# Decoder trunk on one core: gates and mixer up-projections with tokens on the output partitions, and raw buffers of their own for chunks loaded out of turn

## The chip, the cores and the metric

The kernel runs on one core of a Trainium2 chip. The metric is the device time of one execution in microseconds, as the median of several runs. The engines are named as in the profile: PE (matrix multiply; PEld is its weight load), DVE (vector), ACT (scalar), POOL, and SP, whose queue starts most transfers.

## What is computed

Two layers of a decoder trunk over 256 tokens, `D_MODEL` 2048, all in float32. The reference, cut to the part around the change:

```python
def hybrid_mixer(x, ...):
    q, k, v, u = ...                                # x @ w_in, 1024 columns each
    gate_a = jax.nn.sigmoid(x @ w_in[:, OFF_GA:OFF_GS])   # 2048 columns
    gate_s = jax.nn.sigmoid(x @ w_in[:, OFF_GS:])         # 2048 columns
    attn = diff_attention(rope(q), rope(k), v, ...)       # (256, 1024)
    ssm = s5_ssm(u, ..., w_glu)                           # (256, 1024)
    merged = gate_a * (attn @ w_attn_up) + gate_s * (ssm @ w_ssm_up)
    return merged @ w_out

for l in range(2):
    x = layer_norm(ALPHA * x + hybrid_mixer(x, ...), ...)
    h = square(relu(x @ w_mlp_up[l])) @ w_mlp_down[l]
    x = layer_norm(ALPHA * x + h, ...)
```

## The kernel before

Every weight matrix is streamed once from device memory in chunks of 256 input rows by 512 columns (512 KB), laid out as [128, 2, 512]: two k-tiles of 128 rows. A list `plan` holds all chunks in the order of use. `load` takes a raw buffer (tag `w`, 4 buffers), starts the transfer on SP's queue (L344), and has the chunk split into a high and a low part in float32r: ACT writes `hi` (L142), DVE the remainder `lo` (L144). `hi` and `lo` have 3 buffers each. Activations are kept split in the same way, so that one float32 product is three float32r products: high by high, high by low, low by high.

There are two forms of a product with 512 output columns. Both do the same multiplications on a chunk and the same number of PE columns, 6144:

- `gemm_feat` puts features on the output partitions. The weights are the stationary operand, the 256 tokens move: 24 matmuls of 256 columns on a chunk (L532 to L534). The result is [128 features, 256 tokens], in the layout in which the next product takes its activations.
- `gemm_tok` puts tokens on the output partitions (`tok_mul`, L457, L458, L461). The activations are stationary, 128 tokens at a time, and the 512 weight columns move: 12 matmuls of 512 columns on a chunk. The result is [128 tokens, 512 features], once for each half `tt` of the tokens.

A layer runs: `u`, `q`, `k` (feat), `v` (tok), eight gate products (feat, 8 chunks each), four of `w_attn_up` (feat, 4 chunks each), two of `w_glu` (feat), four of `w_ssm_up` (feat, 4 chunks each), `w_out` (tok), a first MLP product (`w_mlp_head`, tok), `w_mlp_up` (`gemm_up`, a third form, L555) and `w_mlp_down` (tok). The gates' evacuation is a tanh on ACT (L968). That of `w_attn_up` (`gate_attn`, L975) multiplies on DVE; that of `w_ssm_up` (`merge`, L1007, L1008, then the split at L142 and L146) makes `merged`, the activations of `w_out`, straight in the layout that `w_out` takes.

Attention and the state-space scan run as background generators on DVE, ACT and a little PE, beside these products: after each chunk, `bg.pump(rate[0])` hands out so many microseconds of background work by the program's own estimate, and `AW` is the share that attention gets against the scan. Whatever attention has left when the gates' products are issued is issued then (`bg.finish(agen)`). A scheduler then places the instructions on each engine.

At the end of `w_out` and of the last `w_mlp_down` of a layer the order of chunks is changed: the last 5 (at the very end 8) chunks of the last product and 2 chunks of the next matrix are taken out of `plan` by `reserve` and loaded ahead, during the two products before (n = 1 and 2, 16 chunks of their own). After each chunk `stash_next` calls `load(own=True)`: the same four raw buffers, but a `whl` slot of its own for `hi` and `lo` (tag `slot`, 17 buffers of 8 KB for each partition, shared with most long-lived tiles). `boundary` and `gemm_tail` use them later. `hold` makes an instruction wait until the last matmul of the most recent chunk is done, and `drip_next` starts a queued POOL transfer (L447) at such a point.

The parts that the change touches:

Of the kernel before, what the change touches and what calls it, by code (L numbers as in the profile page):

```python
# [12 lines left out]
F32R = mybir.dt.float32r  # L13
# [3 lines left out]
ALU = mybir.AluOpType  # L17
# [21 lines left out]
HL_BUFS = 3  # L39
AHEAD = 1  # L40
RATE = (2.0, 1.8)
AW = 1.5
TAIL = 5
LAST = 8
LEAD = 3
# [59 lines left out]
def trunk(ctx: ExitStack, tc: tile.TileContext, A, out):  # L105
# [230 lines left out]
    plan = []  # L336
    ready = []

    def load(w, c, own=False, halves=False):
        kn, wn = w.shape[-2:]  # L340
        raw = wpool.tile([P, kn, wn], F32, tag="w", name=nm("w"), bufs=RAW_BUFS)
        parts = [slice(0, 1), slice(1, 2)] if halves else [slice(0, kn)]
        for k in parts:
            nc.sync.dma_start(raw[:, k], w[c][:, k])  # L344
        if own:
            hl = slot([P, 2, 2, W], F32R, "whl")
            hi, lo = hl[:, 0], hl[:, 1]
        else:
            hi = wpool.tile([P, kn, wn], F32R, tag="whi", name=nm("whi"), bufs=HL_BUFS)
            lo = wpool.tile([P, kn, wn], F32R, tag="wlo", name=nm("wlo"), bufs=HL_BUFS)  # L350
        for k in parts:
            split(hi[:, k], lo[:, k], raw[:, k])
        return hi, lo
# [13 lines left out]

    stash = []
    stashed = {}

    def reserve(w, chunks):
        for c in chunks:
            i = next(i for i, (w_, c_) in enumerate(plan) if w_ is w and c_ == c)
            stash.append(plan.pop(i))

    def stash_next():
        if stash:
            w, c = stash.pop(0)
            stashed[id(w), c] = load(w, c, own=True)

    def take(w, c):
        while any(w_ is w and c_ == c for w_, c_ in stash):
# [80 lines left out]
    def gemm_tok(w, act, nkt, evac, tail=0):  # L463
        ps = banks([P, W])
        nch = nkt // 2
        for c in range(nch - tail):
            hl = take(w, c)
            mm = Chain()
            for tt in range(2):
                tok_mul(mm, ps, act, nkt, hl, c, tt)  # L470
            drip_next(mm.last)
            stash_next()
            bg.pump(rate[0])
        if not tail:
            for tt in range(2):
                evac(tt, ps[tt])
        return ps
# [433 lines left out]
    for l in range(DEPTH):  # L911
# [50 lines left out]
        for base in (G_GS, G_GA):  # L962
            for n in range(4):
                if n % 2 == 0:
                    gt = slot([P, 2, 4, 256], name="gate")
                g = gates[base, n] = gt[:, n % 2]
                gemm_feat(weights("w_in", l, base + n), act, NKT,
                          lambda b, ps: SC.activation(g[:, 2 * b:2 * b + 2, :], ps, AF.Tanh, scale=0.5))  # L968
        bg.finish(agen)
        aact = from_tiles(st["attn"])  # L970
        for n in range(4):
            def gate_attn(b, ps):
                g = gates[G_GA, n][:, 2 * b:2 * b + 2, :]
                with tc.high_priority():
                    V.scalar_tensor_tensor(g, g, 1.0, ps, op0=ALU.add, op1=ALU.mult)  # L975

            gemm_feat(weights("w_attn_up", l, n), aact, 8, gate_attn)
        bg.finish(sgen)
        ghl = []
        for i in range(2):  # L980
# [20 lines left out]
        for n in range(4):  # L1001
            merged.append(slot([P, 4, 2, 256], F32R, "merged"))

            def merge(b, ps):
                bs = slice(2 * b, 2 * b + 2)
                mt = t_fg([P, 2, 256])
                V.scalar_tensor_tensor(mt, gates[G_GS, n][:, bs, :], 1.0, ps, op0=ALU.add, op1=ALU.mult)  # L1007
                V.tensor_tensor(mt, mt, gates[G_GA, n][:, bs, :], op=ALU.add)  # L1008
                split(merged[n][:, bs, 0, :], merged[n][:, bs, 1, :], mt, scale=0.5)

            gemm_feat(weights("w_ssm_up", l, n), sact, 8, merge)
        mact = from_tiles(merged)
        assert not drip
        xgen = None
# [160 lines left out]
```

## Time and profile before

| | before |
|---|---|
| median of 3 runs | 2741.55 us (2741.41 to 2743.21) |
| the profiled execution | 2731.09 us |
| its span, first to last instruction | 2729.3 us |
| PE busy / weight loads busy | 98% / 87% of the span |
| DVE / ACT / POOL busy | 70% / 48% / 5% |
| read from device memory | 513.32 MB |
| mean moved, read and written | 195 GB/s |
| mean granted TensorE clock | 0.994 |

Spans and rows come from the one profiled execution, 10.5 us below the median. A busy share is the union of an engine's instructions. A PE matmul's duration contains its way through the array, which overlaps with the next one, so the distance between starts is what a matmul costs when PE is full.

### The profile page before, as it was taken

What the parts mean: (1) busy time and instruction counts of PE and PEld (TensorE: products, weight loads), DVE (VectorE), ACT (ScalarE), POOL (GpSimd) and SP (SyncE); (2) the same over time, 40 slices, a digit from 0 to 9 for tenths busy, and PEclk for the clock granted to TensorE, in tenths of its full rate; (3) what the DMA queues carried; (4) which work ended last, traced back from release to release, by engine and by line L of the source; (5) the groups of instructions that cost most, each with busy time, mean ns of one, the idle gap of its engine ahead of it and who ended that gap; (6) DMA issues with size and microseconds to landing.
All of it is one profiled execution on the core that took longest, in us unless ns stands there. A gap on an engine that the chain in (4) does not pass through costs nothing. (4 is left out here: it accounts for less than half of the span.)

```text
span 2729.3 us, 41597 instructions
## 1 busy us (share of the span) xinstructions
PE 2676.5 (98%) x16384; PEld 2371.8 (87%) x16384; DVE 1908.7 (70%) x2675; ACT 1312.6 (48%) x1755; POOL 147.1 (5%) x274
## 2 busy tenths in 40 slices
PE   7999999999999999999999999999999999999997
PEld 7889999988888888888789899999788888888876
DVE  6899988676765566655657998987776655556555
ACT  4554555454554454443444555544445544435442
POOL 3100000000000010000012000001000000000000
PEclk9999999999999999999999999999999999999999
DMA  8755555663655676655657555557746555555573
GB/s 262 224 187 188 174 173 169 212 234 122 220 190 192 205 237 212 220 198 195 227 167 253 185 179 171 166 179 230 252 135 205 187 194 191 190 195 186 193 234 121
DMA packets 158675, 536.04 MB, mean 196 GB/s; under 512 B 27504, under 2 KB 27536, under 8 KB 158480
## 3 DMA queue, kind: packets, MB, share of 16 engines
q1 hardware_dynamic: 133344, 482.40, 53.2%
q0 software_dynamic: 25136, 50.99, 6.6%
q8 instruction: 128, 2.10, 0.3%
q14 instruction: 67, 0.55, 0.1%
HBM read 513.32 MB, written 19.92 MB: 195 GB/s over the span
## 5 line engine op out<-in xcount | busy, mean ns | idle before, releaser
L144 DVE TENSOR_TENSOR wlo<-w,whi 128x1024 fp32r<-128x1024 f32 (+1 forms) x884 | 1078.3, 1221 | 660.3 <-ACT whi L142 655.3
L142 ACT ACTIVATE whi<-w 128x1024 fp32r<-128x1024 f32 (+1 forms) x884 | 934.3, 1058 | 1085.3 <-PE g L461 425.6
L555 PE MATMUL g<-xT,whi 128*128 128x512 f32 x1920 | 655.7, 395 | 2.3 <-ACT whi L142 2.3
L532 PE MATMUL g<-xT,whi 128*128 128x256 f32 x1792 | 509.3, 287 | 11.8 <-ACT whi L142 11.8
L533 PE MATMUL g<-xT,whi 128*128 128x256 f32 x1792 | 508.5, 286 | 0.0
L534 PE MATMUL g<-xT,wlo 128*128 128x256 f32 x1792 | 500.0, 287 | 7.1 <-DVE wlo L144 7.0
L555 PE MATMUL g<-xT,wlo 128*128 128x256 f32 x1920 | 497.7, 280 | 0.2 <-DVE wlo L144 0.2
L555 PEld LDWEIGHTS g<-xT,whi 128*128 128x128 f32 x1920 | 344.9, 188 | 66.9 <-ACT whi L142 2.6
L458 PE MATMUL g<-wlo,hT 128*128 128x512 f32 x972 | 379.4, 390 | 3.6 <-DVE wlo L144 3.5
L555 PEld LDWEIGHTS g<-xT,wlo 128*128 128x128 f32 x1920 | 362.1, 189 | 21.7 <-DVE wlo L144 1.4
L457 PE MATMUL g<-whi,hT 128*128 128x512 f32 x972 | 379.1, 390 | 0.9 <-ACT whi L142 0.9
L532 PEld LDWEIGHTS g<-xT,whi 128*128 128x128 f32 x1792 | 347.9, 194 | 14.7 <-ACT whi L142 12.9
L534 PEld LDWEIGHTS g<-xT,wlo 128*128 128x128 f32 x1792 | 341.8, 194 | 10.2 <-DVE wlo L144 9.6
L533 PEld LDWEIGHTS g<-xT,whi 128*128 128x128 f32 x1792 | 347.9, 194 | 1.0 <-issue 0.8
L461 PE MATMUL g<-whi,hT 128*128 128x512 f32 x972 | 300.3, 390 | 0.0
L458 PEld LDWEIGHTS g<-wlo,hT 128*128 128x128 f32 x972 | 182.7, 188 | 43.9 <-DVE wlo L144 5.7
L457 PEld LDWEIGHTS g<-whi,hT 128*128 128x128 f32 x972 | 182.9, 188 | 39.6 <-ACT whi L142 2.1
L461 PEld LDWEIGHTS g<-whi,hT 128*128 128x128 f32 x972 | 182.9, 188 | 38.0
L458 PE MATMUL g<-wlo,merged 128*128 128x512 f32 x216 | 85.3, 395 | 3.4 <-DVE wlo L144 3.2
L560 ACT ACTIVATE at<-g 128x256 f32<-128x256 f32 x120 | 43.8, 384 | 87.3 <-PE g L555 87.3
L457 PE MATMUL g<-whi,merged 128*128 128x512 f32 x216 | 84.4, 391 | 0.0
L710 DVE TENSOR_TENSOR_SCAN sw<-ss,sw 128x512 f32<-128x512 f32 x64 | 75.7, 1212 | 0.0
(290 smaller groups left out, 3186.1 us busy)
## 6 DMA issues: line engine op xcount, KB each, us to landing
w<-in_w_mlp_down_dram SPq DMA_DIRECT2D x256, 512.0 KB, 3.3
w<-in_w_in_dram SPq DMA_DIRECT2D x255, 512.0 KB, 3.4
w<-in_w_mlp_up_dram SPq DMA_DIRECT2D x240, 512.0 KB, 3.3
w<-in_w_out_dram SPq DMA_DIRECT2D x64, 512.0 KB, 4.3
w<-in_w_attn_up_dram SPq DMA_DIRECT2D x32, 512.0 KB, 3.3
w<-in_w_ssm_up_dram SPq DMA_DIRECT2D x32, 512.0 KB, 4.3
w<-in_w_glu_dram SPq DMA_DIRECT2D x16, 512.0 KB, 3.2
w<-in_w_mlp_head_dram SPq DMA_DIRECT2D x16, 512.0 KB, 3.5
```

The lines of the kernel that those rows point to most:

```text
L142: SC.activation(hi, src, AF.Copy, scale=scale)
L144: V.tensor_tensor(lo, src, hi.bitcast(F32), op=ALU.subtract)
L457: mm(PE.matmul(ps[tt], act(kt)[:, 0, ts], hi[:, k, :], start=kt == 0, stop=False))
L458: mm(PE.matmul(ps[tt], act(kt)[:, 0, ts], lo[:, k, :], start=False, stop=False))
L461: mm(PE.matmul(ps[tt], act(kt)[:, 1, ts], hi[:, k, :], start=False, stop=kt == nkt - 1))
L532: m(PE.matmul(o, wh, ah, start=first and b % 2 == 0, stop=False))
L533: m(PE.matmul(o, wh, al, start=False, stop=False))
L534: m(PE.matmul(o, wl, ah, start=False, stop=last and b % 2 == 1))
L555: mm[j](PE.matmul(o, wt, mv, start=kt == 0 and i == 0, stop=last and i == 1))
L560: SC.activation(r[:, j], ps[j][:, 0, :], AF.Copy)
L710: V.tensor_tensor_scan(wv, rg, wv, 0.0, ALU.mult, ALU.add)
```

## The change

The eight gate products, the four of `w_attn_up` and the four of `w_ssm_up` of each layer go from `gemm_feat` to `gemm_tok`. Gates become [tokens, features]. `merge` therefore transposes its result on PE, four 128x128 blocks for each half of the tokens, before the split writes `merged`; the split now reads the transposed block from PSUM. `AW` goes from 1.5 to 1.75. Chunks loaded out of turn no longer use the four raw buffers: `stash_raw` loads them two at a time into a slot of their own (`sraw`), no earlier than the last matmul issued before it, and `stash_turn` splits one after every second chunk instead of one after each.

```diff
--- before.py
+++ after.py
@@ -39,7 +39,7 @@
 HL_BUFS = 3
 AHEAD = 1
 RATE = (2.0, 1.8)
-AW = 1.5
+AW = 1.75
 TAIL = 5
 LAST = 8
 LEAD = 3
@@ -336,18 +336,14 @@
     plan = []
     ready = []
 
-    def load(w, c, own=False, halves=False):
+    def load(w, c, halves=False):
         kn, wn = w.shape[-2:]
         raw = wpool.tile([P, kn, wn], F32, tag="w", name=nm("w"), bufs=RAW_BUFS)
         parts = [slice(0, 1), slice(1, 2)] if halves else [slice(0, kn)]
         for k in parts:
             nc.sync.dma_start(raw[:, k], w[c][:, k])
-        if own:
-            hl = slot([P, 2, 2, W], F32R, "whl")
-            hi, lo = hl[:, 0], hl[:, 1]
-        else:
-            hi = wpool.tile([P, kn, wn], F32R, tag="whi", name=nm("whi"), bufs=HL_BUFS)
-            lo = wpool.tile([P, kn, wn], F32R, tag="wlo", name=nm("wlo"), bufs=HL_BUFS)
+        hi = wpool.tile([P, kn, wn], F32R, tag="whi", name=nm("whi"), bufs=HL_BUFS)
+        lo = wpool.tile([P, kn, wn], F32R, tag="wlo", name=nm("wlo"), bufs=HL_BUFS)
         for k in parts:
             split(hi[:, k], lo[:, k], raw[:, k])
         return hi, lo
@@ -367,16 +363,37 @@
 
     stash = []
     stashed = {}
+    raws = []
+    due = [0]
 
     def reserve(w, chunks):
         for c in chunks:
             i = next(i for i, (w_, c_) in enumerate(plan) if w_ is w and c_ == c)
             stash.append(plan.pop(i))
+        due[0] = 0
+        stash_raw()
+
+    def stash_raw():
+
+        if len(raws) < 2 and len(raws) < len(stash):
+            t = slot([P, 2, 2, W], name="sraw")
+            for i, (w, c) in enumerate(stash[len(raws):len(raws) + 2]):
+                hold(nc.sync.dma_start(t[:, i], w[c]))
+                raws.append(t[:, i])
 
     def stash_next():
         if stash:
             w, c = stash.pop(0)
-            stashed[id(w), c] = load(w, c, own=True)
+            hl = slot([P, 2, 2, W], F32R, "whl")
+            hi, lo = hl[:, 0], hl[:, 1]
+            split(hi, lo, raws.pop(0))
+            stashed[id(w), c] = hi, lo
+            stash_raw()
+
+    def stash_turn():
+        due[0] += 1
+        if due[0] % 2 == 0:
+            stash_next()
 
     def take(w, c):
         while any(w_ is w and c_ == c for w_, c_ in stash):
@@ -469,7 +486,7 @@
             for tt in range(2):
                 tok_mul(mm, ps, act, nkt, hl, c, tt)
             drip_next(mm.last)
-            stash_next()
+            stash_turn()
             bg.pump(rate[0])
         if not tail:
             for tt in range(2):
@@ -962,19 +979,19 @@
         for base in (G_GS, G_GA):
             for n in range(4):
                 if n % 2 == 0:
-                    gt = slot([P, 2, 4, 256], name="gate")
+                    gt = slot([P, 2, 2, W], name="gate")
                 g = gates[base, n] = gt[:, n % 2]
-                gemm_feat(weights("w_in", l, base + n), act, NKT,
-                          lambda b, ps: SC.activation(g[:, 2 * b:2 * b + 2, :], ps, AF.Tanh, scale=0.5))
+                gemm_tok(weights("w_in", l, base + n), act, NKT,
+                         lambda tt, ps: SC.activation(g[:, tt, :], ps, AF.Tanh, scale=0.5))
         bg.finish(agen)
         aact = from_tiles(st["attn"])
         for n in range(4):
-            def gate_attn(b, ps):
-                g = gates[G_GA, n][:, 2 * b:2 * b + 2, :]
+            def gate_attn(tt, ps):
+                g = gates[G_GA, n][:, tt, :]
                 with tc.high_priority():
                     V.scalar_tensor_tensor(g, g, 1.0, ps, op0=ALU.add, op1=ALU.mult)
 
-            gemm_feat(weights("w_attn_up", l, n), aact, 8, gate_attn)
+            gemm_tok(weights("w_attn_up", l, n), aact, 8, gate_attn)
         bg.finish(sgen)
         ghl = []
         for i in range(2):
@@ -1001,14 +1018,18 @@
         for n in range(4):
             merged.append(slot([P, 4, 2, 256], F32R, "merged"))
 
-            def merge(b, ps):
-                bs = slice(2 * b, 2 * b + 2)
-                mt = t_fg([P, 2, 256])
-                V.scalar_tensor_tensor(mt, gates[G_GS, n][:, bs, :], 1.0, ps, op0=ALU.add, op1=ALU.mult)
-                V.tensor_tensor(mt, mt, gates[G_GA, n][:, bs, :], op=ALU.add)
-                split(merged[n][:, bs, 0, :], merged[n][:, bs, 1, :], mt, scale=0.5)
-
-            gemm_feat(weights("w_ssm_up", l, n), sact, 8, merge)
+            def merge(tt, ps):
+                mt = t_fg([P, 4, P])
+                mf = mt.rearrange("p a b -> p (a b)")
+                V.scalar_tensor_tensor(mf, gates[G_GS, n][:, tt, :], 1.0, ps, op0=ALU.add, op1=ALU.mult)
+                V.tensor_tensor(mf, mf, gates[G_GA, n][:, tt, :], op=ALU.add)
+                pt = aux((P, 4, P))
+                for k in range(4):
+                    PE.transpose(pt[:, k, :], mt[:, k, :], ident)
+                ts = slice(tt * P, tt * P + P)
+                split(merged[n][:, :, 0, ts], merged[n][:, :, 1, ts], pt, scale=0.5)
+
+            gemm_tok(weights("w_ssm_up", l, n), sact, 8, merge)
         mact = from_tiles(merged)
         assert not drip
         xgen = None
```

What moves on the engines, in rows of the instruction order that the scheduler makes. A row names line, operation, written tile, read tiles and shape; the numbers behind a tile's name tell instances apart.

PE in layer 0, second product of `w_ssm_up` (`g` is its output in PSUM, `sgl` its activations), where the third chunk begins. Before, there is nothing between its matmuls:

```order
L533 MATMUL g_6146<-sgl_5739,whi_6149 128x256
L534 MATMUL g_6146<-sgl_5739,wlo_6150 128x256
L532 MATMUL g_6145<-sgl_5740,whi_6180 128x256
L533 MATMUL g_6145<-sgl_5740,whi_6180 128x256
L534 MATMUL g_6145<-sgl_5740,wlo_6181 128x256
```

Now, at the same place:

```order
L475 MATMUL g_5148<-wlo_5152,sgl_4779 128x512
L478 MATMUL g_5148<-whi_5151,sgl_4779 128x512 x2
L474 MATMUL g_5147<-whi_5170,sgl_4780 128x512
L1028 MATMUL aux_5129<-ident,at_5126 128x128 x4
L1028 MATMUL aux_5139<-ident,at_5136 128x128 x4
L475 MATMUL g_5147<-wlo_5171,sgl_4780 128x512
```

The eight transposes of the first product stand two chunks and one matmul behind that product's last matmul, in one block, in the middle of the second one.

PE in layer 0, where the last attention result (`ahl`, transposed into `aux`) is made during `w_attn_up`. Before:

```order
L534 MATMUL g_5238<-ahl_2606,wlo_5272 128x256
L810 MATMUL aux_3807<-ident,at_3768 128x128
L532 MATMUL g_5238<-ahl_2606,whi_5271 128x256
L810 MATMUL aux_3807<-ident,at_3768 128x128
L533 MATMUL g_5238<-ahl_2606,whi_5271 128x256
```

Now:

```order
L475 MATMUL g_4546<-wlo_4568,ahl_2594 128x512
L478 MATMUL g_4546<-whi_4567,ahl_2594 128x512 x2
L827 MATMUL aux_3479<-ident,at_3432 128x128 x4
L474 MATMUL g_4469<-whi_4509,ahl_2594 128x512
L475 MATMUL g_4469<-wlo_4510,ahl_2594 128x512
```

Before, the transposes stand 2.4 chunks into `w_attn_up` and the matmuls around them read other rows of `ahl`. Now they stand 6 chunks in, and the matmul behind them (the fourth chunk of the first product, `g_4469`) reads what ACT and DVE make of them. The first three chunks of the second product (`g_4545`, `g_4546`) have been moved ahead of it.

ACT at the last `w_mlp_down` of layer 1, products n = 1 and 2 (`whi` is a chunk's high part in turn, `whl` that of a chunk loaded out of turn). Before:

```order
L142 ACTIVATE whi_25209<-w_25207 128x1024
L142 ACTIVATE whl_25271<-w_25269 128x1024
L142 ACTIVATE whi_25228<-w_25226 128x1024
L142 ACTIVATE whi_25253<-w_25251 128x1024
L142 ACTIVATE whl_25294<-w_25292 128x1024
L142 ACTIVATE whi_25276<-w_25274 128x1024
```

Now, the last part of it:

```order
L142 ACTIVATE whi_23251<-w_23249 128x1024
L142 ACTIVATE whl_23267<-sraw_23141 128x1024
L142 ACTIVATE whl_23306<-sraw_23228 128x1024
L142 ACTIVATE whl_23339<-sraw_23228 128x1024
L142 ACTIVATE whi_23272<-w_23270 128x1024
```

The splits out of turn are spread over both products and read `sraw`, but they still stand ahead of splits in turn on ACT.

## Rows read from the trace of the kernel before

**Rows 1.** Page, part 1: busy time of each engine, share of the span, instructions.

```profile
PE 2676.5 (98%) x16384; PEld 2371.8 (87%) x16384; DVE 1908.7 (70%) x2675; ACT 1312.6 (48%) x1755; POOL 147.1 (5%) x274
```

**Rows 2.** Stretches: length, then busy time (instructions) of PE, PEld, DVE, ACT, POOL, clock, DMA share, GB/s.

```profile
core 0: us, PE busy (x) PEld busy (x) DVE busy (x) ACT busy (x) POOL busy (x), PEclk, DMA share, GB/s
833.50:920.60 87.10, 87.10 (x386) 72.12 (x385) 45.03 (x43) 35.57 (x36) 0.00 (x0) 1.00 0.58 193
512.80:558.90 46.10, 46.10 (x387) 46.10 (x386) 33.26 (x39) 22.28 (x26) 4.38 (x8) 1.00 0.70 229
```

**Rows 3.** Same view: layer 0's `v`, gates and `w_attn_up`; layer 1's gates.

```profile
174.70:226.60 51.90, 51.45 (x265) 41.01 (x263) 48.89 (x76) 32.27 (x55) 6.12 (x12) 1.00 0.63 197
226.60:441.20 214.60, 214.60 (x1765) 205.14 (x1764) 199.62 (x366) 109.67 (x206) 9.71 (x17) 1.00 0.52 171
441.20:489.80 48.60, 48.60 (x423) 47.54 (x422) 30.91 (x38) 21.44 (x26) 0.00 (x0) 1.00 0.53 177
1571.20:1789.00 217.80, 217.71 (x1786) 207.59 (x1785) 196.86 (x351) 110.41 (x211) 12.26 (x21) 1.00 0.53 173
```

**Rows 4.** Waits of DVE, 226.6 to 441.2: total us, times, longest.

```profile
DVE wlo L144 <- ACT whi L142: 7.4, 8, 1.5
DVE ss L738 <- PE y L731: 3.1, 2, 1.7
DVE sw L692 <- PE bu L685: 2.8, 4, 1.1
...
```

**Rows 5.** Timeline of PE at a layer boundary: start, duration, instruction.

```profile
657.99 0.66 PE L853 MATMUL aux<-ident,x 128*128 128x128 f32 x4 [0.40 <-DVE x L849]
658.40 0.47 PE L457 MATMUL g<-whi,xT 128*128 128x512 f32 x1
658.71 0.39 PE L458 MATMUL g<-wlo,xT 128*128 128x512 f32 x1
```

**Rows 6.** Timeline of DVE, first `merge` of layer 0.

```profile
523.81 1.41 DVE L1007 SCALAR_TENSOR_TENSOR at<-gate,g 128x512 f32<-128x512 f32 x2
525.13 1.29 DVE L1008 TENSOR_TENSOR at<-at,gate 128x512 f32<-128x512 f32 x2
```

**Rows 7.** Timeline of all engines, layer 0's last attention result.

```profile
450.91 0.27 PE L810 MATMUL aux<-ident,at 128*128 128x128 f32 x1
...
451.22 0.69 ACT L813 ACTIVATE ahl<-aux,gsub 128x512 fp32r<-128x512 f32 x1 [0.49 <-PE aux L810]
...
451.99 0.74 DVE L814 SCALAR_TENSOR_TENSOR ahl<-aux,gsub,ahl 128x512 fp32r<-128x512 f32 x1
```

**Rows 8.** Waits of all engines, 2640 to 2672, last `w_mlp_down`.

```profile
ACT whl L142 <- DMA w<-in_w_mlp_down_dram: 10.4, 6, 5.2
...
PEld g L458 <- DVE wlo L144: 2.9, 2, 1.9
PE g L458 <- DVE wlo L144: 2.3, 2, 1.5
PEld g L457 <- ACT whi L142: 1.8, 2, 0.9
```

**Rows 9.** Waits of PEld at the other three places, 581:645, 1295:1364, 1930:1995.

```profile
PEld g L458 <- DVE wlo L144: 3.3, 4, 1.1
...
PEld g L458 <- DVE wlo L144: 2.8, 4, 1.1
...
PEld g L458 <- DVE wlo L144: 2.8, 5, 1.1
```

**Rows 10.** Timeline of PE, 2650 to 2657.

```profile
2650.32 0.50 PE L457 MATMUL g<-whi,hT 128*128 128x512 f32 x1 [0.51 <-ACT whi L142]
2652.37 0.50 PE L458 MATMUL g<-wlo,hT 128*128 128x512 f32 x1 [1.54 <-DVE wlo L144]
...
2653.18 1.04 PE L461 MATMUL g<-whi,hT 128*128 128x512 f32 x2
...
2656.58 0.40 PE L457 MATMUL g<-whi,hT 128*128 128x512 f32 x1
```

**Rows 11.** Stretches as in rows 2, around the last out-of-turn loads.

```profile
2627.00:2649.00 22.00, 22.00 (x99) 18.22 (x98) 10.88 (x11) 7.94 (x8) 3.77 (x7) 1.00 0.85 276
2649.00:2660.00 11.00, 8.94 (x31) 6.67 (x30) 7.67 (x7) 6.22 (x7) 0.00 (x0) 0.84 0.80 270
```

## The prediction

> **What bounds the kernel now.** The page's busy shares come first: PE is busy for 98% of the span, the next engine, DVE, for 70% [rows 1]. An average does not tell whether a stage has another limit, so the second view is the table of stretches. In layer 0's gates PE is busy for all of 214.6 us, but DVE is busy for 199.6 of them [rows 3], and DVE's named waits there add 7.4 + 3.1 + 2.8 and some smaller ones [rows 4], so that DVE has nothing left either. There two engines are at their limit; in the other stages that change only PE is. The third view is the timeline of PE at the places where it stops, all in the stretches in which chunks are loaded out of turn [rows 8 to 10].
>
> **Products in the other form.** Both forms send 6144 columns through PE for a chunk, and differ in what a chunk takes. In a stretch with nothing but `tok` products, four of eight chunks, PE has no gap: 87.1 us for 32 chunks, 2.722 us each, 227 ns for a matmul of 512 columns. The four products of `w_ssm_up`, sixteen chunks of `feat`, also without a gap, take 46.1 us, 2.881 us each, 120 ns for a matmul of 256 columns [rows 2]. So 512 columns cost 227 ns in one matmul and 240 in two, and a chunk that changes form saves 0.159 us. Of these there are, in two layers, 2 x 8 x 8 = 128 in the gates, 2 x 4 x 4 = 32 in `w_attn_up` and 32 in `w_ssm_up`: 20.4 + 5.1 + 5.1 = **30.6 us saved**. All of it is on the path wherever PE is the limit.
>
> **Transposes.** `merge` adds 4 on PE for each half of the tokens: 2 layers x 4 products x 2 x 4 = 64, in 16 groups of four. At the layer boundary a group of four of the same shape begins at 657.99 and the matmul behind it at 658.40 [rows 5]: 0.41 us. The ends are 0.23, what a matmul with as many columns takes [rows 2], and 0.66, the whole busy time of the group. I take 0.41, since the next start is what the queue feels: 16 x 0.41 = **6.6 us added** (3.7 to 10.6). So `w_ssm_up` by itself loses 1.5 us.
>
> The Trainium skill ("TensorE: Matmul & The Clock Gate", Part 4: PE-mode transpose) gives some 275 ns for a 128x128 transpose within a kernel. That would be an estimated 17.6 us for 64, and a sum of 17 us instead of 28. The row has 0.41 us for four, so the page's figure is like a duration here and not a cost.
>
> Do the transposes wait for DVE? `w_ssm_up`'s first product begins at 512.80 [rows 2] and ends four chunks later, at 524.3; the second addition of `merge` runs from 525.13 for 1.29 us [rows 6], so its result stands 2.1 us behind the product. In the new order the transposes come two chunks and one matmul behind it, 5.7 us. That leaves 3.6 us, and I cost the wait at nothing. Without that cover, each us would cost 8 us in all, eight blocks with every matmul behind them. ACT and DVE split out of PSUM afterwards, beside PE; `w_out` needs the last `merged` only in its seventh chunk.
>
> **Evacuations.** tanh, `gate_attn` and `merge`'s two DVE operations keep shape and count. They change nothing.
>
> **New waits in the gates.** PE alone would need 214.6 - 64 x 0.159 = 204.4 us in layer 0, DVE 199.6 plus what it waits. Its waits for `hi` come from PE freeing buffers and shrink with PE; those for the scan's results on PE, 5.9 us [rows 4], shrink only in part. `v` shows what that is like: `tok` chunks with DVE busy for 48.89 of 51.9 us, and PE idle for only 0.45 [rows 3]. DVE at 98% will be a little worse. Between 0 and 10.2 us (nothing saved), I take **3 us**, nearest to the row of `v` scaled to the longer stage. Layer 1 has DVE at 196.9 of a coming 207.6 us, so nothing there.
>
> **The last attention result.** Now PE meets its transposes six chunks into `w_attn_up`, and the next matmul needs their outcome. From the last transpose (450.91) to the end of ACT's copy (451.22 + 0.69) pass 1.0 us, to the end of DVE's part 1.8 us [rows 7]. Before, other matmuls lay there; now PE waits about 1 us, and more if DVE is late. Six chunks of 2.72 us after the gates give 16 us, against 9 at which they stood before, so most lateness is covered. Between 0 and 5 us a layer, I take 1.5: **3 us** in all. The higher `AW` only changes the order on DVE, not its work.
>
> **Loads out of turn.** Now eight chunks out of turn and eight in turn want 16 x 0.524 MB in 8 x 2.72 us, 385 GB/s; the chip shows 276 at a DMA share of 0.85 [rows 11], some 325 at a full one. So ACT, in its fixed order, waits for chunks that nobody needs yet (10.4 us, once 5.2), with `hi` and `lo` of the next chunk behind it [rows 8]. PE's weight loads wait 2.9 + 1.8 us there and 3.3, 2.8 and 2.8 at the other three places [rows 8, 9], 13.6 in all. After the longest wait the granted clock of the stretch falls to 0.84 [rows 11], and eight matmuls take from 2653.18 to 2656.58, 3.40 us instead of 1.82 [rows 10]: the 1.2 GHz level. Together 15.2 us at most, and about 14 since a weight load's wait is not all lost.
>
> Spread over both products, 24 chunks want 12.6 MB in 43.5 us, 289 GB/s; `sraw` leaves the four raw buffers to the chunks in turn, and most of its pairs have two or more chunks of time to land. But 289 is near the most seen, the first pair starts when it is nearly due, and ACT still has three splits out of turn in a row near the very end. Between 0 and 15 us, I take **10 us saved**. The new transfers wait on SP for PE; what is queued behind them is 4 raw buffers and 3 split chunks ahead of its use, so I cost that at nothing.
>
> **Sum.** -30.6 + 6.6 + 3 + 3 - 10 = -28.0 us. Against the profiled execution's 2731.1 us that is 2703.1; the median of the runs shown is 10.5 us higher, and the same saving gives **2713.5 us**.
>
> **Rivals.**
> *DVE is the limit of both gate stages.* For it: DVE's busy time and waits fill layer 0's stage. Against it: half of the waits hang on PE. Then the 20.4 us and the 3 us for new waits go: -5.1 - 5.1 + 6.6 + 3 - 10 = -10.6, **2731 us**. Chance 10%.
> *The stops at the out-of-turn loads stay*, with ACT waiting for `sraw` as it does for the raw buffers now. For it: the splits still stand ahead of those in turn. Against it: 289 GB/s instead of 385. Then -18, **2723.5 us**. Chance 10%.
> *The 13 ns go with the columns and not with the matmul.* If 512 columns took 240 ns in these stages in either form, 30.6 us would be lost: +2.6, **2744 us**, no change that can be measured. Against it: rows 2 show both spacings in one kernel, and `v` shows `tok` beside background work. Chance 3%.
> The Trainium skill (same page, Back-to-back issue gap) has N / 2.4 GHz + 2.5 ns for a warm matmul: 215.8 ns and 2 x 109.2, an estimated 6 us for all 192 chunks. The rows have 227 and 240, so the cost for each matmul is larger here than the page's.
> *Slower: PE stops for DVE in the gates, and each stop costs the clock too.* In the trace a stop of 2.05 us (0.51 + 1.54) was followed by the lower clock for 1.6 us more than the work [rows 10]: 3.6 us each. 28 us are used up by eight; ten give +8, **2750 us**. For it: DVE at 98%. Against it: `v`, at 94%, has no such stop, and DVE's whole need is not above today's time. Chance 2%.
> That the change does not do what it says is out: the new order has the `tok` rows.
>
> **How the numbers follow.** The forecast has 75%. With all four uncertain costs at their lower ends at once (3.7, 0, 0, -15) it would be 2700, with all at their upper ends (10.6, 10.2, 10, 0) 2742; they hardly meet there, and half of each distance gives 2707 to 2728. The range holds that, reaches to 2702 below for three of the four at their lower ends, and to 2731 above for the first two rivals. A measurement of this kernel tells 0.2%, 5.5 us, from no change. Below 2736 lie the forecast, two rivals and nearly all between them: faster 0.94, same 0.04, slower 0.02.
>
> **What would show it.** Right: gate stages of 205 to 209 us, matmuls 227 ns apart in them; `w_attn_up` 47 to 49 us; `w_ssm_up` 46.5 to 48 us with transposes in groups of 0.4 us; 64 more PE transposes and 4608 of the 256-column matmuls replaced by 2304; weight loads' waits at the four out-of-turn places below 5 us in all. Wrong: a gate stage above 212 us with waits of PE for `wlo`, transposes that wait for DVE, or ACT waiting for `sraw` with PE behind it.

## The result, and the profile after

| | before | after |
|---|---|---|
| median of 4 runs each, same chip | 2741.48 us (2739.34 to 2743.21) | 2714.91 us (2705.79 to 2716.31) |
| ratio of the two | | 0.9896, 95% interval 0.9873 to 0.9920 |
| profiled execution: time, span | 2731.09, 2729.3 us | 2716.07, 2714.1 us |

The change saves 26.6 us by the medians; 28.0 were forecast, as 2713.5 us in a range of 2702 to 2731. The prediction was right. The profiled executions differ by 15.2 us of span only: the one of before was 10 us faster than that kernel's runs, the one of after 1 us slower than its median. The table below divides those 15.2 us; the second profile of the kernel further down shows which part of it belongs to the change.

The page of after, part 1, busy time of each engine, as in [rows 1]:

```profile
PE 2648.8 (98%) x14144; PEld 2254.0 (83%) x14144; DVE 1906.6 (70%) x2675; ACT 1307.5 (48%) x1755; POOL 147.1 (5%) x274
```

16384 matmuls became 14144: 4608 fewer, 2304 and 64 more, as announced. PE works 27.7 us less. But its span shrank by 15.2 us, so it stands idle for 12.5 us more.

Stretches of after, columns as in [rows 2]: layer 0's gates, `w_attn_up`, `w_ssm_up`; layer 1's gates and `w_attn_up`; 11 us among the last loads out of turn.

```profile
229.70:432.80 203.10, 203.10 (x991) 162.80 (x990) 194.38 (x349) 107.70 (x197) 9.70 (x17) 1.00 0.59 180
432.80:482.80 50.00, 47.94 (x238) 37.92 (x237) 36.13 (x55) 22.54 (x35) 0.00 (x0) 1.00 0.58 178
505.80:552.10 46.30, 46.30 (x219) 38.57 (x218) 32.87 (x39) 21.50 (x26) 4.37 (x8) 1.00 0.72 228
1570.30:1776.30 206.00, 206.00 (x1003) 163.75 (x1002) 194.13 (x339) 107.56 (x197) 12.26 (x21) 1.00 0.59 183
1776.30:1831.80 55.50, 50.96 (x245) 40.01 (x244) 42.61 (x73) 25.11 (x42) 0.00 (x0) 0.97 0.51 159
2639.00:2650.00 11.00, 11.00 (x50) 9.11 (x49) 8.31 (x7) 7.21 (x8) 0.00 (x0) 1.00 1.02 373
```

In both gate stages PE is still busy for all of the time, in layer 0 with 991 matmuls where 1765 stood [rows 3]. `w_attn_up` is the stage that got longer: 50.0 and 55.5 us, with PE idle for 2.1 and 4.5 of them. From the first matmul of a stage to the first of the next (layer 0's `u` from the start of the span):

| stretch | before | after | difference |
|---|---|---|---|
| `v`, gates, `w_attn_up`, layer 0 | 315.08 | 305.03 | -10.05 |
| the same, layer 1 | 294.37 | 289.19 | -5.18 |
| `w_ssm_up`, both layers | 92.90 | 92.70 | -0.2 |
| the four out-of-turn stretches | 541.43 | 528.86 | -12.6 |
| `u`, `q`, `k` of both layers, second part of `w_mlp_up` of layer 0 | 416.66 | 429.81 | +13.1 |

The four out-of-turn stretches are, in each layer, `w_out` and the last two of the four parts of `w_mlp_down`, which follow each other. The last line is work that the change does not touch. Most of what is longer there are waits of PE behind transfers. Waits of PE between 40 and 180 us (total, times, longest), of after and then of a second set of runs of the same kernel (`change_again`):

```profile
PE g L549 <- ACT whi L142: 10.3, 1, 10.3
PE bu L702 <- DMA us<-usplit: 4.0, 1, 4.0
```

```profile
PE bu L702 <- DMA us<-usplit: 8.1, 2, 7.8
...
PE g L549 <- ACT whi L142: 2.2, 2, 1.9
```

The wait for `whi` takes 10.3 us in one execution of the program and 2.2 in all in another (in after ACT was itself waiting for a chunk, 13.1 us long), while the one for `usplit` grows from 4.0 to 8.1. In all PE waits 16.1 us there in after, 13.8 in `change_again` and 12.1 in before; in layer 1 (1400 to 1572 us) 10.1, 5.7 and 3.8. So a good part of the last line changes from execution to execution.

The weight-load waits at the four out-of-turn places, 13.6 us before [rows 8, 9], are 0.7, 0, 0.2 and 0 us now. Waits of all engines of after around the last of them (2626:2660):

```profile
ACT whl L142 <- DMA sraw<-in_w_mlp_down_dram: 3.3, 3, 1.5
```

ACT still waits for `sraw`, 3.3 us in this window and 6.7 in the whole stretch, instead of 10.4 in either, and no wait of PE or PEld is left in the answer.

### The profile page after: what moved, and what is told of

Read it like the earlier page. It is cut to its first block, busy times and chain, and to the rows that moved or that the text cites. A ratio compares the mean times of both kernels' runs of the same rounds, so it can differ in the third digit from the quotient of the medians.

```text
span 2714.1 us, 37124 instructions
## 1 busy us (share of the span) xinstructions
PE 2648.8 (98%) x14144; PEld 2254.0 (83%) x14144; DVE 1906.6 (70%) x2675; ACT 1307.5 (48%) x1755; POOL 147.1 (5%) x274
## 5 line engine op out<-in xcount | busy, mean ns | idle before, releaser
L572 PE MATMUL g<-xT,wlo 128*128 128x256 f32 x1920 | 497.9, 280 | 1.5 <-DVE wlo L144 1.5
L572 PEld LDWEIGHTS g<-xT,whi 128*128 128x128 f32 x1920 | 345.1, 188 | 68.2 <-ACT whi L142 3.9
L572 PEld LDWEIGHTS g<-xT,wlo 128*128 128x128 f32 x1920 | 362.2, 189 | 23.1 <-DVE wlo L144 2.8
L475 PE MATMUL g<-wlo,xT 128*128 128x512 f32 x680 | 267.7, 394 | 0.5 <-DVE wlo L144 0.5
L474 PE MATMUL g<-whi,xT 128*128 128x512 f32 x680 | 265.5, 392 | 0.0
L549 PE MATMUL g<-xT,whi 128*128 128x256 f32 x768 | 218.6, 288 | 18.1 <-ACT whi L142 18.1
L551 PE MATMUL g<-xT,wlo 128*128 128x256 f32 x768 | 213.9, 289 | 5.6 <-DVE wlo L144 5.5
L550 PE MATMUL g<-xT,whi 128*128 128x256 f32 x768 | 218.1, 287 | 0.0
L478 PE MATMUL g<-whi,xT 128*128 128x512 f32 x680 | 211.5, 391 | 0.0
L549 PEld LDWEIGHTS g<-xT,whi 128*128 128x128 f32 x768 | 150.7, 196 | 19.1 <-ACT whi L142 19.0
L551 PEld LDWEIGHTS g<-xT,wlo 128*128 128x128 f32 x768 | 147.4, 197 | 7.8 <-DVE wlo L144 7.5
L550 PEld LDWEIGHTS g<-xT,whi 128*128 128x128 f32 x768 | 150.9, 197 | 0.0
L475 PEld LDWEIGHTS g<-wlo,xT 128*128 128x128 f32 x680 | 128.0, 188 | 27.3 <-issue 1.2
```

What stands on the lines that cost most here:

```text
L474: mm(PE.matmul(ps[tt], act(kt)[:, 0, ts], hi[:, k, :], start=kt == 0, stop=False))
L475: mm(PE.matmul(ps[tt], act(kt)[:, 0, ts], lo[:, k, :], start=False, stop=False))
L478: mm(PE.matmul(ps[tt], act(kt)[:, 1, ts], hi[:, k, :], start=False, stop=kt == nkt - 1))
L549: m(PE.matmul(o, wh, ah, start=first and b % 2 == 0, stop=False))
L550: m(PE.matmul(o, wh, al, start=False, stop=False))
L551: m(PE.matmul(o, wl, ah, start=False, stop=last and b % 2 == 1))
```

## The experiments

All ratios are to the kernel before, run on the same chip as the kernel in the line (7 to 15 runs, medians 2737.46, 2741.27 and 2740.95 us). Lengths of stretches are from one profiled execution each.

| kernel | median us | ratio, 95% interval |
|---|---|---|
| `loads_only` | 2727.65 | 0.9961 (0.9944 to 0.9978) |
| `products_only` | 2722.43 | 0.9944 (0.9926 to 0.9962) |
| `pace_only` | 2723.68 | 0.9947 (0.9927 to 0.9967) |
| `buffers_only` | 2709.54 | 0.9904 (0.9877 to 0.9932) |
| `six_raws` | 2751.94 | 1.0042 (1.0028 to 1.0056) |
| `twice` | 2717.14 | 0.9915 (0.9896 to 0.9934) |
| `no_td` | 2712.54 | 0.9894 (0.9876 to 0.9913) |
| `pool_td` | 2727.74 | 0.9955 (0.9940 to 0.9970) |
| `aw15` | 2712.15 | 0.9889 (0.9873 to 0.9905) |
| `carry` | 2721.50 | 0.9931 (0.9916 to 0.9947) |
| `carry_each` | 2722.24 | 0.9933 (0.9921 to 0.9946) |
| `change_again` | 2711.98 | 0.9893 (0.9879 to 0.9906) |

### The two parts by themselves

`loads_only` is the kernel before with the change's hunks in `load`, `reserve`, `stash_next` and the products' call of `stash_turn`, and nothing else. `products_only` is the change with the old loads:

```diff
-            split(hi, lo, raws.pop(0))
-            stashed[id(w), c] = hi, lo
-            stash_raw()
+            stashed[id(w), c] = load(w, c, own=True)
...
-            stash_turn()
+            stash_next()
```

> The loads out of turn as in the change, everything else as before (products in the old form, AW 1.5). My theory: PE's stops in the four out-of-turn stretches (13.6 us of weight-load waits and some 1.6 us of lower clock in the trace of before) nearly vanish by this part alone, so 2741.5 - 13 = 2728.5 us, and the gate stages stay at 214.6 and 217.8 us. Rival, that the stops went because PE's products before them are in another form and the weights run ahead further: the stops stay, 2741 us.

> The products in the new form with AW 1.75, the loads out of turn as before. My theory: the two parts add, so this has the rest of the change, 2741.5 - 14 = 2727.5 us, with the weight loads' waits at the four out-of-turn places at 12 to 15 us as before, and the waits of PE at the last attention result as in the changed kernel (w_attn_up 50 and 55.5 us). Rival, that the two parts help or hinder each other: more than 5 us away from that.

With the loads alone the four stretches go from 541.43 to 527.77 us, and `v`, gates and `w_attn_up` stay at 315.14 and 294.63. With the products alone the four stretches stay (540.63) and the gates' stretches are 305.08 and 287.73, as in the change. Each part acts in its own place. The ratios multiply to 0.9905 beside the 0.9896 of the whole: 0.39% is 10.7 us for the loads, 0.56% is 15.3 us for the products. Waits around the last loads, of `products_only` (2620:2680), show the old stop:

```profile
ACT whl L142 <- DMA w<-in_w_mlp_down_dram: 10.1, 7, 2.8
...
PEld g L458 <- DVE wlo L144: 3.7, 5, 1.1
...
PEld g L457 <- ACT whi L142: 1.5, 2, 0.8
```

### What in the loads does it: the pace, or buffers of their own

The prediction gave two reasons, and held the pace (every second chunk, 289 instead of 385 GB/s) to be the main one. `pace_only` keeps the pace and gives back the shared raw buffers; `buffers_only` keeps the buffers and loads one in every chunk.

```diff
# pace_only: stash_next
-            split(hi, lo, raws.pop(0))
+            stashed[id(w), c] = load(w, c, own=True)
...
# buffers_only: stash_turn
-        if due[0] % 2 == 0:
-            stash_next()
+        stash_next()
```

> The changed kernel, but the chunks out of turn go through the four shared raw buffers again; only the pace of one for every two chunks is kept. My theory: what made the stops is that two chunks for each 2.72 us want 385 GB/s and ACT waits in its order for a chunk that is not yet needed; the pace alone takes 289 GB/s, so at least two thirds of the 13 us are saved: at most 4 us more than the changed kernel's 2715. Rival, that the shared buffers made the stops: the stops stay, 2725 us or more.

> The changed kernel, with raw buffers of its own for the chunks out of turn, but one of them after every chunk as before. My theory (pace): 385 GB/s are wanted again, the stops stay, weight loads wait 10 us or more at the four places, 2725 us. Rival (buffers): the stops stay away, 2715 us.

The four stretches take 544.78 us with the pace alone, worse than before, and 528.11 with buffers alone, as good as the change. The reason given for the loads fell, and the rival holds. Waits of `pace_only`, 2635:2675, and of SP's queue there:

```profile
ACT whl L142 <- DMA w<-in_w_mlp_down_dram: 16.0, 6, 3.4
```

```profile
SPq L344 <- DVE whl L144: 12.8, 6, 2.3
```

ACT waits even longer for loads out of turn, 16.0 us instead of 10.4 [rows 8], although half as many of them are wanted at a time. SP's transfers wait 12.8 us there for raw buffers that hold chunks out of turn not yet split; in after (2626:2660) none waits for such a split. Bandwidth isn't the cause either. A stretch of `buffers_only` in the same place, columns as before, and its wait (2615:2650):

```profile
2640.00:2650.00 10.00, 10.00 (x46) 8.29 (x45) 9.90 (x11) 6.55 (x8) 0.00 (x0) 1.00 1.00 384
```

```profile
ACT whl L142 <- DMA sraw<-in_w_mlp_down_dram: 6.9, 4, 3.2
```

384 GB/s flow at full speed of PE, which is what the old pace asks for. The prediction had scaled [rows 11], 276 GB/s at a DMA share of 0.85, up to 325, and took that for a ceiling. There is none at 325, and the trace of before had it already, in layer 1's `u`, `q`, `k`:

```profile
1445.00:1455.00 10.00, 10.00 (x86) 10.00 (x85) 8.34 (x11) 5.51 (x8) 5.90 (x9) 1.00 1.02 366
```

`six_raws` separates "more raw buffers for the chunks in turn" from "a separate place for those out of turn": `products_only` with six shared raw buffers, for which one of the 17 `slots` had to go.

```diff
-RAW_BUFS = 4
+RAW_BUFS = 6
...
-    slots = ctx.enter_context(tc.tile_pool(name="slots", bufs=17))
+    slots = ctx.enter_context(tc.tile_pool(name="slots", bufs=16))
```

> Products in the new form, loads out of turn as before (one after every chunk, in the shared raw buffers), but six shared raw buffers instead of four, and one long-lived slot fewer to make room. Theory after the last runs: the stops come because the chunks out of turn take two of four raw buffers from those in turn, so that these are loaded late; with six the stops nearly vanish, weight loads wait below 4 us at the four places and the four stretches take 529 us in all as in the changed kernel. Rival, that only transfers held until the product before is done keep the queue in good order: the stretches stay at 541 us. The missing slot may lengthen other stages, which tells nothing on this.

`v`, gates and `w_attn_up` are 26 to 29 us longer (331.25 and 316.63 us where `products_only` has 305.08 and 287.73), so the total says nothing on the loads; the missing slot is the likely cause, which no run shows by itself. The four stretches do say something: 529.98 us, as with `sraw`, with weight-load waits of 0.4 to 0.7 us in each place. Shared buffers are enough if there are six.

Sums over the four stretches, in us, of what ACT waited for chunks in turn and out of turn, and of what PE's weight loads waited for `hi` and `lo` (16.1 in before, as the windows are wider than in [rows 8, 9]):

| kernel | ACT, in turn | ACT, out of turn | weight loads |
|---|---|---|---|
| before | 24.5 | 35.9 | 16.1 |
| `products_only` | 26.4 | 34.7 | 14.4 |
| `pace_only` | 3.9 | 86.3 | 17.4 |
| `six_raws` | 0.5 | 43.4 | 2.3 |
| `loads_only` | 0 | 24.5 | 2.5 |
| after | 0 | 25.5 | 0.9 |

ACT's wait for chunks that nobody needs yet is longer in `six_raws` than in before, and PE hardly stops. So that wait alone is not what stops PE; the number of raw buffers is. With four shared ones, each chunk out of turn takes one of the four until it is split; with six, SP's queue still waits for such splits (10.7 us in 2655:2690), but has two buffers more to fill. Whether the chunks in turn must have four to themselves, or whether six of any kind would do in every case, these runs don't tell apart.

### The transposes

`twice` makes every transpose of `merge` two times, the second over the first.

```diff
-                for k in range(4):
+                for k in (0, 1, 2, 3, 0, 1, 2, 3):
```

> The changed kernel with every transpose of merge done twice (64 more in all). My theory: a group of four costs PE 0.41 us and nothing waits, so w_ssm_up grows by 4 x 2 x 0.41 = 3.3 us in each layer at most (from 46.25 to 49.5; 2.7 by the difference to 16 chunks of 2.722 us in the changed kernel, so 49), the total by 5 to 7 us. Rival, that their cost is the wait for DVE or a fixed one for each place: w_ssm_up grows by under 1 us.

Timeline of PE (start, duration, instruction) in the second product of layer 0's `w_ssm_up`, of after and then of `twice`:

```profile
522.37 1.03 PE L1028 MATMUL aux<-ident,at 128*128 128x128 f32 x8
523.16 0.47 PE L475 MATMUL g<-wlo,sgl 128*128 128x512 f32 x1
```

```profile
523.74 1.91 PE L1028 MATMUL aux<-ident,at 128*128 128x128 f32 x16
525.40 0.47 PE L475 MATMUL g<-wlo,sgl 128*128 128x512 f32 x1
```

No bracket with a wait stands behind any of these lines: the transposes wait for nothing. Eight more take 525.40 - 523.74 = 1.66 instead of 0.79 us, 0.87 us. The stage agrees: it got 2.62 and 2.68 us longer, for six of the eight groups, since the last two lie in `w_out` (the first block of `w_out`'s matmuls stands at 552.05, the transposes of the fourth product at 557.72). That is 0.44 us for a group of four, some 7 us for the change's 16. The page of the Trainium skill that was weighed against this ("TensorE: Matmul & The Clock Gate", Part 4: PE-mode transpose, some 275 ns each) agrees with the duration of one, 272 ns in this trace; as a cost for each of 64 the runs rule it out.

### The last attention result

`w_attn_up` should have gained 2.5 us by the products and lost 1.5. It lost 1.4 in layer 0 (48.56 to 49.96) and 6.6 in layer 1 (48.93 to 55.52), and some of PE's background work from the gates was pushed into it (some 6 matmuls in layer 0, 15 in layer 1). Waits of PE of after, layer 1's `w_attn_up` (1776.3:1831.8):

```profile
PE y L748 <- DVE sw L736: 1.5, 1, 1.5
PE g L475 <- DVE wlo L144: 1.2, 1, 1.2
```

and the timeline of PE there:

```profile
1795.95 0.61 PE L478 MATMUL g<-whi,ahl 128*128 128x512 f32 x2
1798.08 2.18 PE L748 MATMUL y<-sw,cz 128*32 128x256 f32 x32 [1.51 <-DVE sw L736]
1800.95 1.10 PE L827 MATMUL aux<-ident,at 128*128 128x128 f32 x4 [0.70 <-ACT at L822]
1802.83 0.50 PE L474 MATMUL g<-whi,ahl 128*128 128x512 f32 x1 [0.78 <-ACT ahl L830]
...
1804.37 0.63 PE L474 MATMUL g<-whi,ahl 128*128 128x512 f32 x1
1804.79 0.63 PE L475 MATMUL g<-wlo,ahl 128*128 128x512 f32 x1
```

PE, after a stop of 1.2 us for a late split of weights, has done the six chunks that don't need the last attention result, and then stops three times in a row: for a product that reads the scan's result, for the transposes' input, and for the outcome. Behind the stops matmuls start 0.42 us apart, the 1.2 GHz level, and the granted clock of the stretch is 0.97. In `change_again` the same stops are as long, but the clock stays at 1.00 and the stage takes 53.94 us: the lower clock costs 1.6 us, and not in every execution. DVE's timeline tells why the input (`at`, written by ACT at line 822 from 1800.53 on) was late:

```profile
1789.61 0.16 DVE L817 TENSOR_SCALAR ss<-ss 128x4 f32<-128x4 f32 x1
...
1795.53 0.15 DVE L332 TENSOR_TENSOR rsa<-rs 128x4 f32<-128x4 f32 x1
1795.60 0.68 DVE L735 TENSOR_TENSOR sw<-sw,e_re 128x512 f32<-128x512 f32 x1
1796.20 1.22 DVE L144 TENSOR_TENSOR wlo<-w,whi 128x1024 fp32r<-128x1024 f32 x1
1797.34 0.68 DVE L736 TENSOR_TENSOR sw<-ss,ss 128x512 f32<-128x512 f32 x1
1797.94 0.15 DVE L333 SCALAR_TENSOR_TENSOR rsa<-rsa,ss 128x4 f32<-128x4 f32 x1
1798.02 0.68 DVE L737 TENSOR_TENSOR sw<-sw,ss 128x512 f32<-128x512 f32 x1
1798.62 1.22 DVE L144 TENSOR_TENSOR wlo<-w,whi 128x1024 fp32r<-128x1024 f32 x1
1799.75 0.15 DVE L334 SCALAR_TENSOR_TENSOR rs<-rsa,rs 128x4 f32<-128x4 f32 x1
...
1800.33 0.16 DVE L334 SCALAR_TENSOR_TENSOR rs<-rsa,rs 128x4 f32<-128x4 f32 x1
```

The norm of the last attention result is a chain of eleven steps of some 0.15 us (lines 817 and 326, then three times lines 332 to 334, iterations of an inverse square root). Most of them stand in DVE's order one by one between steps of the scan and splits of weights, so that 1.7 us of work take from 1789.61 to 1800.49.

Five kernels try this. `no_td` leaves one product of the scan out, of the state's real part and `e_re` (16 instructions of 0.68 us in a layer), so what comes out is another state-space result. `pool_td` makes the same product on POOL. `aw15` sets back the weight that decides between attention and scan. `carry` takes 24 small DVE instructions out of a layer, by multiplying the carried state with `s_r` when it is copied. `carry_each` is that and `buffers_only` together.

```diff
# no_td
-                V.tensor_tensor(td, s[0], er, op=ALU.mult)
...
-                V.tensor_tensor(s[0], td, ta, op=ALU.subtract)
+                V.tensor_tensor(s[0], tb, ta, op=ALU.subtract)
# pool_td
-                V.tensor_tensor(td, s[0], er, op=ALU.mult)
+                GP.tensor_tensor(td, s[0], er, op=ALU.mult)
# aw15
-AW = 1.75
+AW = 1.5
# carry
-                        V.tensor_tensor(carry[:, ri, :], carry[:, ri, :], s_r[:, lp + 8 * g:lp + 8 * g + 8], op=ALU.mult)
...
-                        V.tensor_copy(carry[:, ri, :], s[ri][:, :, L - 1])
+                        V.tensor_tensor(carry[:, ri, :], s[ri][:, :, L - 1], s_r[:, lp + 8 * g:lp + 8 * g + 8], op=ALU.mult)
```

> The changed kernel with less DVE work in the scan: of the six DVE products and sums after each scan step one (the product of the state's real part with e_re, 16 in a layer, 0.6 us each) is left out, its place taken by another operand, so the scan's result is another. My theory: what PE waits for in w_attn_up is DVE's work, which now lasts longer than PE's; with 9.7 us less of it in a layer, w_attn_up goes from 50.0 and 55.5 us to 48 and 49 us, and the total to 2707. Rival, that the last attention result is late by the length of its own chain of small steps over the engines: both stages stay, 2715.

> The changed kernel with that product moved from DVE to POOL, which is 5% busy; the result is the reference's. My theory: DVE gets 9.7 us a layer back; if POOL needs under 2 us for one and does not slow DVE, w_attn_up falls to 48 and 49 us and the total to 2707; if POOL is much slower or takes DVE's time, the scan's chain gets longer, the gain is gone and w_attn_up grows. Rival, the chain of attention: 2715 as the changed kernel.

> The changed kernel with AW at 1.5 as before. My theory: AW only shifts attention against the scan, DVE's work is the same and ends as late; layer 0's order is the same, w_attn_up within 1 us of 50.0 and within 2 us of 55.5, total 2715. Rival, that the higher AW holds the attention's end back from being later still: w_attn_up longer by 3 us or more.

> The changed kernel with 24 small DVE instructions fewer in a layer: the scan's carry is multiplied where it is copied. My theory: DVE's work up to the last attention result is what PE waits for, so gates and w_attn_up lose what these took, 1.8 us (75 ns each in a row of small ones) to 3.9 us (160 ns each) a layer where PE still waits, about 1.5 in layer 0 and 2 to 3.5 in layer 1. Rival: no more than 0.5 us in either.

> The same, with one split out of turn after every chunk instead of every second one (own raw buffers as in the change). Expected to be as carry or up to 1 us better, since the pace was shown to matter little; it would be the fastest, about 2709 us.

`no_td`: `v`, gates and `w_attn_up` take 303.54 and 285.70 us, 1.5 and 3.5 less than in the change. PE's waits before the end of layer 1's `w_attn_up` (1740:1832) shrink to

```profile
PE g L474 <- ACT ahl L829: 0.8, 1, 0.8
PE g L475 <- DVE wlo L144: 0.3, 1, 0.3
```

so some 9 us less of DVE's busy time in a layer (1889.3 us in all instead of 1906.6) remove most of the stops. In layer 1 the transposes still stand behind six chunks, so there DVE's load is the likely cause of the stops. In layer 0 the scheduler also moved them up, to 21 matmuls into the stage, and much of the background work into the stages before (`v` and gates 4.5 us longer): `w_attn_up` is 44.02 and 50.47 us where 48 and 49 were expected. In the total, 0.9894, this can't be told from the change. `pool_td` shows that moving the product to POOL costs more than it frees. The line's group in `pool_td` (xcount, busy, mean ns, idle before) and in after:

```profile
L733 POOL TENSOR_TENSOR ss<-sw,e_re 128x512 f32<-128x512 f32 x32 | 66.7, 2085 | 317.1 <-DVE sw L727 278.8 <-DVE rs L334 20.0 <-DVE sw L724 9.9
```

```profile
L733 DVE TENSOR_TENSOR ss<-sw,e_re 128x512 f32<-128x512 f32 x32 | 21.9, 683 | 0.0
```

With 2085 ns instead of 683 on the scan's own path the stretches are 311.81 and 294.23 us, and the kernel is slower than the change. PE's instructions stand at the same places of `w_attn_up` as in `no_td`, so in layer 1 a slower scan makes 8.5 us at the same order of PE. `aw15` costs 2.3 us in layer 1 (291.46; `w_attn_up` 57.75, between what the theory and its rival said) and none in layer 0 (304.99); the total does not tell it from the change.

`carry` was to help and did not: layer 0 gained 0.7 us, layer 1 lost 6.8 (295.97), and the total is worse than the change's, 0.9931 beside 0.9893. PE in layer 1's `w_attn_up`, and DVE before it:

```profile
1796.84 0.39 PE L810 MATMUL aux<-v,wT 128*128 128x128 f32 x2
1802.18 1.25 PE L826 MATMUL aux<-ident,at 128*128 128x128 f32 x4 [4.95 <-ACT at L821]
```

```profile
1798.44 0.17 DVE L816 TENSOR_SCALAR ss<-ss 128x4 f32<-128x4 f32 x1 [0.95 <-ACT at L814]
...
1801.50 0.16 DVE L334 SCALAR_TENSOR_TENSOR rs<-rsa,rs 128x4 f32<-128x4 f32 x1
```

DVE is even idle before the chain (0.95 us), and the eleven steps take only 3.2 us here, from 1798.44 to 1801.66, but they begin later, since the scheduler has put the last attention result later. PE then waits 4.95 us in one piece. How late the order puts it can be counted in layer 1: the last matmuls that make this result (L810 here, `aux<-v,wT`) stand behind 36 matmuls of `w_attn_up` in `no_td`, 37 in after, 49 in `aw15` and all 72 of the six chunks in `carry`; PE's wait for the transposes' input is 0, 0.7, 3.3 and 4.95 us. So the amount of DVE work is one part of the cause, and the other is where the order puts the last chain, with six chunks of PE as its cover. How much each part costs is not shown, since an edit that changes the one changes the other too. `carry_each` has the same stop in layer 1 (`w_attn_up` 64.25 us, `carry` 64.22), and its total, 0.9933, is `carry`'s.

### The change once more

> The changed kernel once more, without an edit, to see what its time does by itself. Expected: median 2712 to 2717 us; the stages from the first gate to the end of w_attn_up as long as before to 0.3 us, while the stages that the change does not touch and that share the memory with the many small transfers of the scan's operands (u, q, k of both layers and w_mlp_up's second part) differ by several us. If instead these stages stay as in the first profile, the 13 us that they were longer than in the kernel before belong to the change.

Ratio 0.9893, with 2708.47 to 2714.65 us in four runs. In its profiled execution, of 2706.4 us span, `v`, gates and `w_attn_up` take 304.94 and 287.67 us; `u`, `q` and `k` are shorter by 3.4 and 4.0 us than in the first profile of the same kernel. So some 7 of the 13.1 us in the table's last line come and go between executions. Two expectations failed: layer 1's stretch differs by 1.5 us, not 0.3 (the clock above), and the 3 us in `w_mlp_up` came again (97.14 us after 97.19, before 94.18). They don't come with the change: that part takes 97.94 us in `loads_only`, 94.21 in `pace_only` and 93.80 in `carry`. What sets it was not tried.

## Why the prediction was right, point by point

**Products, 30.6 us saved: right.** The 0.159 us of a chunk are what the stages show. `w_ssm_up` has 16 chunks, 2.54 us less, and six groups of transposes, and came out 0.17 longer in layer 0. The gates with `v` are 11.4 and 11.8 us shorter, 10.2 by the rule; the rest is background work of PE that now lies in `w_attn_up`. The stage lengths were to be 205 to 209 us, and the gates take 203.1 and 206.0 us, layer 0's less than was said for the same reason. That the saving comes with fewer matmuls, and not with the tokens on the output partitions, a stage of before shows in which the weights stay the stationary operand, the second part of layer 1's `w_mlp_up`, with 256 matmuls of 512 and 256 of 256 columns:

```profile
2269.50:2358.90 89.40, 89.40 (x514) 78.09 (x512) 54.06 (x62) 46.52 (x61) 0.00 (x0) 1.00 0.56 189
```

That is 349 ns for a pair, where three matmuls of 256 columns would take 360: 11 of the 13 ns are gained without a change of form.

**Transposes, 6.6 us: right, slightly small.** 0.44 us for a group instead of 0.41, 7 us in all, and no wait for DVE. `w_ssm_up` was put at 46.5 to 48 us and measured 46.25 and 46.45, because a quarter of its transposes falls into `w_out`.

**New waits in the gates, 3 us: wrong, there are none.** PE is busy for all of both stages. DVE's waits in layer 0's gates (total, times, longest):

```profile
DVE wlo L144 <- ACT whi L142: 3.4, 5, 0.9
...
DVE sw L709 <- PE bu L702: 2.6, 4, 0.9
```

The wait for `hi`, 7.4 us before [rows 4], has more than halved, as the prediction said it would where PE frees buffers sooner; the one for `bu` stayed at 2.6 of 2.8. The rival in which DVE limits both gate stages is refuted by this.

**The last attention result, 3 us: right mechanism, too small.** This is the term that was mis-sized. PE stops where it was said to, after six chunks, and the link that was priced, from the transposes to the next matmul [rows 7], costs 1.3 and 0.8 us of wait, near the 1.5. What was missed is what comes before that link. With DVE at 96 and 94% in the gates the rest is late too, and PE also waits for splits of weights (0.7 and 1.2 us), in layer 1 for the scan (1.5) and for the transposes' input (0.7). Against the 12.7 us that PE's arithmetic gives to a layer, `v`, gates and `w_attn_up` gained 10.05 and 5.18 in the first profile, 10.1 and 6.7 in the second: short by 2.6 and 6 to 7.5, some 9 us in two layers beside the 3 + 3 forecast for both waits.

**Loads out of turn, 10 us saved: right size, wrong reason.** `loads_only` gives 10.7 us, within 6 and 15 by its interval; the stops fell from 13.6 to 0.9 us where less than 5 was forecast. But the pace that was held to be the main cure does nothing by itself, the ceiling of 325 GB/s does not exist (the trace that the prediction read has 366), and ACT's wait for chunks that nobody needs yet is longest but one in `six_raws`, which hardly stops. What counts is how many raw buffers there are.

**The sum.** By the runs the parts are some -30.6 + 7 + 9 - 10.7 = -25.3 us, where 26.6 were measured and 28.0 forecast. The single terms are off by up to 6 us and partly cancel; that the sum is off by only 1.4 us is in part luck. The rivals with PE stopping for DVE in the gates, and with stops that stay at the loads, did not happen.

## What to carry to other kernels

Count the matmuls and not only their columns: where each is fed with new weights, as here, each one fewer at the same columns was worth 11 to 13 ns, and a transposition behind them was cheap (0.44 us for four) where it stood two chunks after what it reads; nearer was not tried. When loads out of turn stop an engine, look first at whose buffers they hold and how many there are, before bandwidth and pace. And where the work that covers a chain of small steps gets shorter, price the chain as it runs in its real place in the busy engine's order, not as it runs when that engine is free.

## What was not expected

One core moved 384 GB/s for 10 us while PE was at full speed, where the rows that were read for the prediction had 276 GB/s. A DMA share of 0.85 therefore doesn't give a ceiling by division: in `buffers_only` the share is 1.00 at 341 GB/s (2630:2640) and at 384.

Two executions of one program differ by up to 10.5 us (2705.79 and 2716.31). Between the two that were profiled, 2716.07 and 2708.47 us, `u`, `q` and `k` with their waits behind transfers make the difference. Layer 1's `u`, `q` and `k`, which the change leaves alone, took 7.1 us longer in the first profile than in before, as much as all the transposes cost; in the profiles of the experiments they take 0.8 to 7.9 us longer than in that one execution of before.

24 DVE instructions fewer in a layer made the kernel slower than the change by 0.4%, through the order that the scheduler then chose.
